# Down projection as seven products in passes over the chunks, with two weight sums formed in memory

## The chip, the cores and the metric

The kernel runs on one core of one Trainium2 chip. The metric is device microseconds of one execution; lower is better. Engines are called as the profile calls them: PE (TensorE), PEld (its weight loads), DVE (VectorE), ACT (ScalarE), POOL (GpSimd) and SP (SyncE, which issues most loads here).

## The reference

One layer of an encoder on 512 tokens of 2048 features, in float32. Three groups of attention heads read one normalised input; their output goes through a projection and is added to x. Then comes the gated MLP, the part that matters here:

```
h = rmsnorm(x, ffn_norm)                          # 512 x 2048
g = causal_dwconv(h @ w_gate, conv_w, conv_b)     # 512 x 5632, width 3
u = h @ w_up                                      # 512 x 5632
x = x + (silu(g) * u) @ w_down                    # 5632 -> 2048: "down"
return rmsnorm(x, final_norm)
```

## The kernel before, in words

Activations are kept transposed: features lie on the 128 partitions, the 512 tokens along the row. To reach float32 precision, each operand is split into a high and a low part in a reduced format (`split`, L57): ACT copies it with rounding into the high part (L58) and DVE subtracts that from the operand (L59). One product of two tiles is then three matmuls (`mm3`, L61: high times low, low times high, high times high, all at L64).

The program runs in stages. The attention stage (heads `n` = 0 to 15; the first 8 are differential, then 4 stick-breaking pairs, then 4 band pairs) weaves the small matmuls of one head with the big projections of the following head (`weave`); the order on PE is that in which the program writes them, the order on the other engines is set by a planner that places each instruction where it expects its inputs and buffers to be ready. POOL takes part in the heads: it negates the row maximum of each softmax block (L375) and masks triangles in the stick heads (L506). Then come the output projection (`wo`), gate and up, and down.

Gate and up work on 44 tiles `f` of 128 hidden features. The first four are plain products of 512 columns. The other 40 (`strassen`, L799) take the weights of gate and up and the halves of tokens and contraction as 2x2 blocks and form seven products of 256 columns in place of eight. Their weight sums are formed on the way in by accumulating loads (L808) and by DVE (L819). At the end of each `f` the result `u` (a part of the tile `g`) is multiplied with the activated gate `cv` (L881) and written to `a_dram` on POOL's queue (L882). The tiles `g`, `cv`, `U`, `X` are in the pool `fp`, the weights in the five tiles of the pool `r4`, all opened for this stage and closed at its end. Pools are stacked: one that is opened after others have closed lies on their bytes.

Down takes the 44 hidden tiles as 11 chunks of 4 (`CH`, `NCH`). `gated(c)` loads a chunk of features (1 MB) from `a_dram` into a tile of the pool `wraw` and splits it into the tiles `ah`, `al`, in the pool `big`. `down` walks over four groups `g` of weights (1 MB each, `load_unit`) and in each over four tiles of 128 output features: 4 hidden tiles x 3 matmuls of 512 columns into one PSUM bank `dn`, and one addition into `x2` (L930). `x2` holds x after attention; its eight tiles take the place of `sums_`, the input sums of the gate stage, and are loaded at the boundary on POOL's queue (L971). The tiles `h2h` and `h2l` of the pool `h2p` hold the other inputs of the gate stage (`second`). The last chunk is done in two halves of tokens, so that the final norm of the first half can begin early.

Weights pass through two raw tiles (`wraw`) and three pairs of split tiles (`wh`, `wl` of the pool `wspl`, 1024 columns each).

Of the kernel before, what the change touches and what calls it, by code (L numbers as in the profile page):

```python
# [41 lines left out]
def trunk(ctx, tc, xT, wqkv, wo, wo15, wgu, wd, par, lam4, rel, out):  # L42
# [41 lines left out]
    def att_bank(name="att"):  # L84
        return ps_att.tile([P, S], F32, tag="att", name=name)
# [152 lines left out]
    with ExitStack() as actx:  # L238
# [110 lines left out]
        def block_scores(qkh, c, i, bank):  # L349
# [4 lines left out]
            pe.matmul(bank[:, kt], q[c][:, qt], k[c][:, kt], start=True, stop=False)  # L354
            pe.matmul(bank[:, kt], q[c][:, qt], kh[c][:, kt], start=False, stop=True)  # L355

        UOFF = [0, 128, 384, 768]

        def softmax_block(qkh, c, i, bias, dst, sums, n):

            w = (i + 1) * P
            bank = att_bank("sc")
            block_scores(qkh, c, i, bank)
            mx = sm.tile([P, 1], F32, tag="mx", name="mx")
            dve.tensor_tensor_reduce(
                out=dst,
                in0=bank[:, 0:w],
                in1=bias[:, S - w : S],
                op0=ALU.add,
                op1=ALU.max,  # L370
                scale=1.0,
                scalar=NEG,
                accum_out=mx,
            )
            pool.tensor_scalar(out=mx, in0=mx, scalar1=-1.0, scalar2=None, op0=ALU.mult)  # L375
            act.activation(dst, dst, AF.Exp, bias=mx, accum_out=sums[:, n : n + 1])

        def transposed(w):
# [122 lines left out]
        def stick_pair(p, qkh, vs):  # L501
            def strictly_before(t, fill):

                for i in range(NB):
                    o = UOFF[i] + i * P
                    pool.affine_select(  # L506
                        out=t[:, o : o + P],
                        in_=t[:, o : o + P],
                        pattern=[[-1, P]],
                        compare_op=ALU.is_gt,  # L510
                        fill=fill,
                        base=0,
                        channel_multiplier=1,
                    )
# [35 lines left out]
        ready, vtiles, pending = {}, {}, []  # L550

        def unit_order():
            yield from (HEADS_AT, HEADS_AT + 1)
# [149 lines left out]
    with ExitStack() as actx:  # L703
# [31 lines left out]
        def plain(f):  # L735
# [14 lines left out]
            pool.dma_start(a_dram[:, f, :], u)  # L750

# [44 lines left out]
            )  # L796
            return parts_of(h2p, "h2", j, b, 3)

        def strassen(f, first=False):  # L799
# [72 lines left out]
            product(halves(a12), second, 2, bank2[:, lo], False, False)  # L872
            product(halves(a22), sums_, 3, bank2[:, hi], False, True)
            dve.tensor_tensor(
                out=g[:, 2 + HS : 2 + HS + S].rearrange("p (a b) -> p a b", b=HS),
                in0=bank2.rearrange("p (a b) -> p a b", b=HS),
# [2 lines left out]
            )  # L879
            cv, silu = convolved(f, g)  # L880
            dve.scalar_tensor_tensor(out=u, in0=u, scalar=-1.0, in1=cv, op0=ALU.mult, op1=ALU.mult)  # L881
            pool.dma_start(a_dram[:, f, :], u)  # L882
            return silu

        NPLAIN = 4
# [3 lines left out]
                sums_ = [sums(j) for j in range(KT // 2)]  # L889
        second = [blocks(j) for j in range(KT // 2)]  # L890
        for f in range(NPLAIN, NFT):
            silu = strassen(f, f == NPLAIN)


    with ExitStack() as actx:
        fp = actx.enter_context(tc.tile_pool(name="fp", bufs=2))
        x2 = None

        def gated(c):

            raw = wraw.tile([P, CH, S], F32, tag="raw", name="araw")
            sync.dma_start(raw, a_dram[:, c * CH : (c + 1) * CH, :])
            ah, al = [], []
            for i in range(CH // 2):
                j = (c % 2) * 2 + i
                h, l = [big.tile([P, 2, S], F32R, tag=f"b{x}{j}", name=f"a{x}") for x in "hl"]
                split(h, l, raw[:, 2 * i : 2 * i + 2, :])
                ah += [h[:, n, :] for n in range(2)]
                al += [l[:, n, :] for n in range(2)]
            return ah, al  # L910

        ssum3 = h2p.tile([P, S], F32, tag="ssum", name="ssum3")

# [49 lines left out]
                    yield  # L963
            yield

        a = gated(0)
        x2 = []
        for j in range(4, 8):
            for x in "hl":
                t = big.tile([P, 2, S], F32, tag=f"b{x}{j}", name="x2")  # L970
                pool.dma_start(t, x_dram[:, len(x2) : len(x2) + 2, :])  # L971
                x2 += [t[:, n, :] for n in range(2)]
# [7 lines left out]
        t0, t1 = slice(0, S // 2), slice(S // 2, S)  # L980

        kept = [
            [h2p.tile([P, 1024], F32R, tag=f"h2{x}{i}", name=f"k{x}{i}") for x in "hl"] for i in range(8)
        ]
        kept = [kept[2 * g : 2 * g + 2] for g in range(4)]
        down((load_unit(wd[NCH - 1, g], kept[g]) for g in range(4)), a, t0, squares)
# [72 lines left out]
```

## Time and profile before

| | |
|---|---|
| median of 3 runs | 2275.19 us (2273.24 to 2277.32) |
| profiled execution, its own time | 2275.25 us |
| its span, first to last instruction | 2273.5 us |
| mean granted PE clock | 0.99 |
| PE busy | 2215.1 us, 97% of the span |
| DVE, ACT, POOL busy | 1530.2, 993.1, 286.8 us |
| moved by DMA | 333 MB, mean 147 GB/s |

A row of a group reads: line, engine, operation, output <- inputs, shapes, xcount, then busy time and mean ns of one, then idle time of the engine just before these instructions and what ended it. A row of a window has its length, the busy time of each engine with the number of instructions, the granted clock, the share of time in which the DMA engines were busy, and GB/s. A row of a tile gives shortest, median and longest duration in ns and the start of the first and the last instruction. A row of the timeline starts with the start time and the duration. A row of DMA issues ends with KB each and the median us from issue to landing.

### The profile page before, as it was taken

What the parts mean: (1) busy time and instruction counts of PE and PEld (TensorE: products, weight loads), DVE (VectorE), ACT (ScalarE), POOL (GpSimd) and SP (SyncE); (2) the same over time, 40 slices, a digit from 0 to 9 for tenths busy, and PEclk for the clock granted to TensorE, in tenths of its full rate; (3) what the DMA queues carried; (4) which work ended last, traced back from release to release, by engine and by line L of the source; (5) the groups of instructions that cost most, each with busy time, mean ns of one, the idle gap of its engine ahead of it and who ended that gap; (6) DMA issues with size and microseconds to landing.
All of it is one profiled execution on the core that took longest, in us unless ns stands there. A gap on an engine that the chain in (4) does not pass through costs nothing.

```text
span 2273.5 us, 34753 instructions
## 1 busy us (share of the span) xinstructions
PE 2215.1 (97%) x14012; PEld 2015.8 (89%) x14012; DVE 1530.2 (67%) x2183; ACT 993.1 (44%) x1490; POOL 286.8 (13%) x519
## 2 busy tenths in 40 slices
PE   6999999989999999899999999999999999999997
PEld 6889888878888888689999999999999888888887
DVE  7675766787777547767777777777777655555565
ACT  4554555565565323344444444444444322222232
POOL 5000100221111320001111101111110000000003
PEclk9999999999999999999999999999999999999999
DMA  5222222222234444767787777777775533333332
GB/s 183 86 84 94 87 79 89 79 79 80 98 112 157 160 150 156 232 189 188 196 208 192 195 197 189 203 203 191 198 189 158 213 127 113 130 111 119 140 130 75
DMA packets 79745, 333.07 MB, mean 147 GB/s; under 512 B 9312, under 2 KB 14176, under 8 KB 63200
## 3 DMA queue, kind: packets, MB, share of 16 engines
q1 hardware_dynamic: 57776, 257.84, 34.0%
q0 software_dynamic: 20512, 71.84, 14.2%
q8 instruction: 110, 1.80, 0.3%
q10 hardware_dynamic: 1296, 1.17, 0.2%
q14 instruction: 51, 0.42, 0.1%
HBM read 307.22 MB, written 23.59 MB: 146 GB/s over the span
## 4 chain that ended last, share of the span: by engine, by line
PE 89%; DVE 5%; ACT 2%; DMA 2%; issue 1%; POOL 1%; SPq 0%; POOLq 0%; DVEq 0%; ACTq 0%
PE c L64 35%; PE dn L64 21%; PE wo L64 8%; PE v L64 7%; PE k L64 6%; PE q L64 6%; PE tr L385 1%; DMA xt<-x_dram 1%; PE g L64 1%; DVE wl L59 1%; PE pv L64 1%; PE sc L355 1%; PE sc L354 1%; DVE l L536 1%; POOL z L506 1%
## 5 line engine op out<-in xcount | busy, mean ns | idle before, releaser
L58 ACT CAST wh<-raw 128x1024 fp32r<-128x1024 f32 (+1 forms) x227 | 236.1, 1041 | 504.5 <-PE dn L64 299.8
L64 PE MATMUL c<-bl,wh 128*128 128x256 f32 x1280 | 363.5, 284 | 13.6 <-ACT wh L58 13.6
L59 DVE TENSOR_TENSOR wl<-a,wh 128x1024 fp32r<-128x1024 f32 x200 | 244.6, 1224 | 191.8 <-ACT wh L58 191.7
L64 PE MATMUL c<-bh,wl 128*128 128x256 f32 x1280 | 363.5, 284 | 0.7 <-DVE wl L59 0.7
L64 PE MATMUL c<-bh,wh 128*128 128x256 f32 x1280 | 363.3, 284 | 0.0
L59 DVE TENSOR_TENSOR wl<-raw,wh 128x1024 fp32r<-128x1024 f32 (+1 forms) x227 | 277.3, 1223 | 98.5 <-ACT wh L58 98.1
L58 ACT CAST wh<-a 128x1024 fp32r<-128x1024 f32 x200 | 209.8, 1049 | 245.1 <-DVE a L819 207.6
L64 PE MATMUL c<-h2l,wh 128*128 128x256 f32 x960 | 272.0, 283 | 0.9 <-DVE U L844 0.9
L64 PE MATMUL c<-h2h,wl 128*128 128x256 f32 x960 | 271.8, 283 | 0.0
L64 PE MATMUL c<-h2h,wh 128*128 128x256 f32 x960 | 271.8, 283 | 0.0
L64 PEld LDWEIGHTS c<-bl,wh 128*128 128x128 f32 x1280 | 246.8, 193 | 13.8 <-ACT wh L58 13.8
L930 DVE TENSOR_TENSOR x<-dn,x 128x512 f32<-128x512 f32 (+1 forms) x192 | 123.8, 646 | 187.5 <-PE dn L64 183.4
L64 PE MATMUL dn<-al,wh 128*128 128x512 f32 x640 | 249.2, 389 | 0.8 <-DVE al L59 0.7
L64 PE MATMUL dn<-ah,wl 128*128 128x512 f32 x640 | 249.0, 389 | 0.0
L64 PE MATMUL dn<-ah,wh 128*128 128x512 f32 x640 | 249.0, 389 | 0.0
L64 PEld LDWEIGHTS c<-bh,wl 128*128 128x128 f32 x1280 | 246.8, 193 | 1.0 <-DVE wl L59 1.0
L64 PEld LDWEIGHTS c<-bh,wh 128*128 128x128 f32 x1280 | 246.9, 193 | 0.0
L64 PEld LDWEIGHTS c<-h2l,wh 128*128 128x128 f32 x960 | 184.6, 192 | 1.1 <-DVE U L844 1.1
L64 PEld LDWEIGHTS c<-h2h,wl 128*128 128x128 f32 x960 | 184.5, 192 | 0.0
L64 PEld LDWEIGHTS c<-h2h,wh 128*128 128x128 f32 x960 | 184.4, 192 | 0.0
L64 PE MATMUL v<-wl,hh 128*128 128x256 f32 x512 | 149.3, 292 | 13.1 <-DVE wl L59 12.9
L64 PE MATMUL v<-wh,hl 128*128 128x256 f32 x512 | 147.6, 288 | 4.1 <-DVE hl L59 4.1
(241 smaller groups left out, 4736.4 us busy)
## 6 DMA issues: line engine op xcount, KB each, us to landing
a<-in_wgu SPq DMA_DIRECT2D x120, 512.0 KB, 4.8
raw<-in_wqkv SPq DMA_DIRECT2D x46, 1024.0 KB, 4.8
raw<-in_wd SPq DMA_DIRECT2D x44, 1024.0 KB, 4.9
z<-in_wgu SPq DMA_DIRECT2D x80, 512.0 KB, 5.8
z<-in_wgu POOLq DMA_DIRECT2D x80, 512.0 KB, 9.8
raw<-in_wo SPq DMA_DIRECT2D x16, 1024.0 KB, 4.8
a_dram<-g POOLq DMA_DIRECT2D x44, 256.0 KB, 6.0
araw<-a_dram SPq DMA_DIRECT2D x11, 1024.0 KB, 4.9
```

The source lines that it names most:

```text
L58: act.copy(out=hi, in_=src)
L59: dve.tensor_tensor(out=lo, in0=src, in1=hi.bitcast(F32), op=ALU.subtract)
L64: pe.matmul(o, l[x], r[y], start=start and i == 0, stop=stop and i == 2, skip_group_check=on)
L354: pe.matmul(bank[:, kt], q[c][:, qt], k[c][:, kt], start=True, stop=False)
L355: pe.matmul(bank[:, kt], q[c][:, qt], kh[c][:, kt], start=False, stop=True)
L385: pe.transpose(out=bank[:, (i - j) * P : (i - j + 1) * P], in_=w[:, o : o + P], identity=ident)
L506: pool.affine_select(out=t[:, o : o + P], in_=t[:, o : o + P], pattern=[[-1, P]], compare_op=ALU.is_gt, fill=fill, base=0, channel_multipl ...
L536: dve.tensor_tensor_scan(back, back, back, 0.0, ALU.add, ALU.max)
L930: dve.tensor_tensor(out=x2[m][:, t], in0=bank, in1=x2[m][:, t], op=ALU.add)
```

## The change

Down for chunks 0 to 9 is written as seven products. A pair `q` of chunks gives two column blocks of the weights; the output tiles of each group of weights give two row blocks; the tokens are halved. All products have 256 columns. Product `r` reads one combination of weight blocks and one combination of feature blocks, and is added into one to four of the four output blocks (`INTO`). The products are done in five passes over the five pairs: (5), then (6, 3) together, (4), (1, 7) together, (2). In a pass a product keeps its four PSUM banks over all five pairs, and is added into `x2` only in the last.

The weight sums s1 (row 1, both columns) and s2 (s1 plus row 0, column 0) are formed in DRAM by copies and accumulating transfers on POOL's queue during the attention stage, three a head, 40 in all. The two other sums of weights are formed by DVE. The feature combinations are formed by DVE from blocks of 128 x 1024 in a new pool `ar` of five tiles, and two of them are kept in DRAM (`t1_dram`, `t2_dram`) for later passes. Weights are loaded as two 512 KB tiles that take the places of `h2h` (eight tiles), for the first pair of the first pass as 1 MB into `wraw`. `a_dram` has a new order with the halves of tokens apart, so each write of `u` is in two runs a partition. In the last `f` of the gate stage the order of the last two products is swapped. The last chunk and the final norm are as before, save for which `h2` tiles keep its weights.

```diff
-    a_dram = dram.tile([P, NFT, S], F32, name="a_dram")
+    a_dram = dram.tile([P, 2, NFT, S // 2], F32, name="a_dram")
...
+            last_pool[:] = [pool.tensor_scalar(out=mx, in0=mx, scalar1=-1.0, scalar2=None, op0=ALU.mult).ins]
...
+        def weight_sums():
+            def block(i, row, col):
+                q, g = i // 2, i % 2 * 2
+                return wd[2 * q + col, g : g + 2, :, row * 1024 : (row + 1) * 1024]
+            n = 2 * NQ
+            for i in range(n + 2):
+                if i < n:
+                    yield lambda: pool.dma_start(s1_dram[i], block(i, 1, 0))
+                    yield lambda: pool.dma_start(s2_dram[i], block(i, 0, 0))
+                if 1 <= i < n + 1:
+                    yield lambda: pool.dma_start(s1_dram[i - 1], block(i - 1, 1, 1), accum_op=ALU.add)
+                if 2 <= i:
+                    yield lambda: pool.dma_start(
+                        s2_dram[i - 2], s1_dram[i - 2], accum_op=ALU.add, max_dma_last_dim=1024
+                    )
...
+            marks = [total * x // 4 for x in (1, 2, 3)]
             for w in att:
                 done += w
+                while marks and done >= marks[0]:
+                    marks.pop(0)
+                    issue = next(wsums, None)
+                    if issue is not None:
+                        with tc.issue_after(last_pool[0]):
+                            issue()
...
+            if last:
+                product(halves(a22), sums_, 3, bank2[:, hi], False, False)
+            product(halves(a12), second, 2, bank2[:, lo], False, last)
+            if not last:
+                product(halves(a22), sums_, 3, bank2[:, hi], False, True)
...
+        ar = actx.enter_context(tc.tile_pool(name="ar", bufs=5))
...
+        def block(c, t):
+            b = ar.tile([P, 1024], F32, tag="a", name="ab")
+            sync.dma_start(b, a_dram[:, t, c * CH : (c + 1) * CH, :].rearrange("p a b -> p (a b)"))
+            return b
...
+        def features(r, q):
+            if r in (1, 2, 3):
+                return in_parts(block(2 * q + (r > 1), int(r == 3)))
+            if r == 5:
+                x, y = block(2 * q, 0), block(2 * q, 1)
+                dve.tensor_tensor(out=x, in0=x, in1=y, op=ALU.subtract)
+                pool.dma_start(t1_dram[q], x)
+                return in_parts(x)
+            if r == 7:
+                x, y = block(2 * q + 1, 1), block(2 * q, 1)
+                dve.tensor_tensor(out=x, in0=x, in1=y, op=ALU.subtract)
+                return in_parts(x)
+            x, y = block(2 * q + 1, int(r == 6)), ar.tile([P, 1024], F32, tag="a", name="tb")
+            sync.dma_start(y, (t1_dram if r == 6 else t2_dram)[q])
+            dve.scalar_tensor_tensor(out=x, in0=x, scalar=-1.0, in1=y, op0=ALU.mult, op1=ALU.subtract)
+            if r == 6:
+                pool.dma_start(t2_dram[q], x)
+            return in_parts(x)
...
+        def raw_blocks(src, first):
+            if first:
+                raw = wraw.tile([P, 2, 1024], F32, tag="raw", name="raw")
+                sync.dma_start(raw, src.rearrange("g p n -> p g n"))
+                return [raw[:, g, :] for g in range(2)]
+            tiles = []
+            for g in range(2):
+                raw = h2p.tile([P, 1024], F32, tag=f"h2h{raws[0] % 8}", name="raw")
+                raws[0] += 1
+                sync.dma_start(raw, src[g])
+                tiles.append(raw)
+            return tiles
+
+        def weights(rs, q, g2, first):
+            def a(row, col):
+                return raw_blocks(wd[2 * q + col, 2 * g2 : 2 * g2 + 2, :, row * 1024 : (row + 1) * 1024], first)
+            i = 2 * q + g2
+            srcs = {
+                (5,): lambda: (raw_blocks(s1_dram[i], first),),
+                (6, 3): lambda: (raw_blocks(s2_dram[i], first), a(0, 1)),
+                (4,): lambda: (a(1, 1),),
+                (1, 7): lambda: (a(0, 0), a(1, 0)),
+                (2,): lambda: (a(0, 1),),
+            }[rs]()
+            for g in range(2):
+                ws = []
+                for n, src in enumerate(srcs):
+                    if n:
+                        dve.tensor_tensor(out=src[g], in0=src[g], in1=srcs[0][g], op=ALU.add)
+                    wh = wspl.tile([P, 1024], F32R, tag="wh", name="wh")
+                    wl = wspl.tile([P, 1024], F32R, tag="wl", name="wl")
+                    split(wh, wl, src[g])
+                    ws.append((wh, wl))
+                yield ws
+
+        INTO = {
+            1: ((0, 0), (0, 1), (1, 0), (1, 1)),
+            2: ((0, 0),),
+            3: ((0, 1),),
+            4: ((1, 0),),
+            5: ((0, 1), (1, 1)),
+            6: ((0, 1), (1, 0), (1, 1)),
+            7: ((1, 0), (1, 1)),
+        }
+
+        def one_pass(rs, new_banks, first=False):
+            banks = [[new() for _ in range(4)] for new in new_banks]
+            for q in range(NQ):
+                fs = [features(r, q) for r in rs]
+                for g2 in range(2):
+                    for gg, ws in enumerate(weights(rs, q, g2, first and q == 0)):
+                        g = 2 * g2 + gg
+                        for bank, f, w in zip(banks, fs, ws):
+                            # 2 output tiles x 4 hidden tiles, mm3 of 256 columns each
...
+                        if q == NQ - 1:
+                            # bank g of each product is added into x2 as INTO says
...
-        for c in range(NCH - 1):
-            down((load_unit(wd[c, g]) for g in range(4)), a)
-            a = gated(c + 1)
+        one_pass((5,), (acc,), True)
+        one_pass((6, 3), (acc, dn_bank))
+        one_pass((4,), (dn_bank,))
+        one_pass((1, 7), (acc, dn_bank))
+        one_pass((2,), (acc,))
+        a = gated(NCH - 1)
```

More of the change, by code (lines that the diff above doesn't have):

```diff
@@ L107, in trunk @@
     x_dram = dram.tile([P, KT, S], F32, name="x_dram")
-    a_dram = dram.tile([P, NFT, S], F32, name="a_dram")
+    a_dram = dram.tile([P, 2, NFT, S // 2], F32, name="a_dram")
+    NQ = NCH // 2
+    s1_dram, s2_dram = [
+        [dram.tile([2, P, 1024], F32, name=f"{n}_{i}") for i in range(2 * NQ)] for n in ("s1", "s2")
+    ]
     def feature_tiles(tag, name, dtype=F32R):
@@ L505, in strictly_before @@
                     o = UOFF[i] + i * P
[L506 to L514, printed above, removed]
+                    last_pool[:] = [
+                        pool.affine_select(
+                            out=t[:, o : o + P],
+                            in_=t[:, o : o + P],
+                            pattern=[[-1, P]],
+                            compare_op=ALU.is_gt,
+                            fill=fill,
+                            base=0,
+                            channel_multiplier=1,
+                        ).ins
+                    ]
             zs = []
@@ L897, in trunk @@
         x2 = None
+        ar = actx.enter_context(tc.tile_pool(name="ar", bufs=5))
+        HS = S // 2
+        raws, combs = [0], [0]
         def gated(c):
             raw = wraw.tile([P, CH, S], F32, tag="raw", name="araw")
-            sync.dma_start(raw, a_dram[:, c * CH : (c + 1) * CH, :])
+            for t in range(2):
+                sync.dma_start(raw[:, :, t * HS : (t + 1) * HS], a_dram[:, t, c * CH : (c + 1) * CH, :])
             ah, al = [], []
             for i in range(CH // 2):
[L905 to L909, printed above, removed]
@@ L910, in gated, with comb @@
-            return ah, al
+                h, l = comb()
+                split(h, l, raw[:, 2 * i : 2 * i + 2, :].rearrange("p a b -> p (a b)"))
+                ah += [h[:, n * S : (n + 1) * S] for n in range(2)]
+                al += [l[:, n * S : (n + 1) * S] for n in range(2)]
+            return ah, al
+        def comb():
+            j = combs[0] % 4
+            combs[0] += 1
+            return [big.tile([P, 1024], F32R, tag=f"b{x}{j}", name=f"a{x}") for x in "hl"]
+        x2p = []
@@ new lines, in block, with in_parts @@
+        def block(c, t):
+            b = ar.tile([P, 1024], F32, tag="a", name="ab")
+            sync.dma_start(b, a_dram[:, t, c * CH : (c + 1) * CH, :].rearrange("p a b -> p (a b)"))
+            return b
+        t1_dram, t2_dram = [[dram.tile([P, 1024], F32, name=f"{n}_{q}") for q in range(NQ)] for n in ("t1", "t2")]
+        def in_parts(b):
+            p = comb()
+            split(*p, b)
+            return p
+        def features(r, q):
[16 more added lines that the diff above has]
+            return in_parts(x)
@@ L982, in trunk @@
         kept = [
-            [h2p.tile([P, 1024], F32R, tag=f"h2{x}{i}", name=f"k{x}{i}") for x in "hl"] for i in range(8)
+            [h2p.tile([P, 1024], F32R, tag=f"h2{'lh'[i // 4]}{i % 4 * 2 + n}", name=f"k{n}{i}") for n in range(2)] for i in range(8)
         ]
```

38 lines of the change are left out of this document (30 added, 8 removed).

## The prediction

> **What bounds the kernel now.** I read the page's busy times first, then the windows of the stages, then the instructions of the two stages that meet at the change.
>
> ```profile
> span 2273.5 us, 34753 instructions
> ...
> PE 2215.1 (97%) x14012; PEld 2015.8 (89%) x14012; DVE 1530.2 (67%) x2183; ACT 993.1 (44%) x1490; POOL 286.8 (13%) x519
> ```
>
> ```profile
> core 0: us, PE busy (x) PEld busy (x) DVE busy (x) ACT busy (x) POOL busy (x), PEclk, DMA share, GB/s
> ...
> 46.00:380.00 334.00, 334.00 (x1918) 293.90 (x1917) 214.29 (x478) 173.88 (x347) 29.47 (x94) 1.00 0.26 89
> 380.00:560.00 180.00, 168.94 (x974) 148.62 (x973) 139.13 (x193) 109.18 (x192) 38.44 (x83) 0.97 0.22 77
> ...
> 977.00:1776.00 799.00, 797.69 (x6646) 797.29 (x6644) 581.22 (x632) 366.66 (x437) 93.43 (x155) 1.00 0.73 190
> 1776.00:2212.00 436.00, 435.63 (x1921) 360.53 (x1922) 236.79 (x269) 111.00 (x107) 3.33 (x7) 1.00 0.39 138
> ```
>
> TensorE bounds all of it. The stage that changes is 1776 to 2212 (down for ten chunks): PE is busy 435.6 of 436 us at a granted clock of 1.00, DVE 237, DMA 0.39. The gate and up stage before it (977 to 1776) already works by seven products of 256 columns. Its PE is as full, with DVE at 581 of 799 us (73%), so it is the pattern for what the new down asks of the other engines. Two tiles give the rates:
>
> ```profile
> L64 PE MATMUL dn<-al,wh x640: 389/389/500, 1776.3 to 2211.3; 128*128 128x512 f32 x160
> ...
> L64 PE MATMUL dn<-ah,wh x640: 388/389/393, 1776.8 to 2211.7; 128*128 128x512 f32 x160
> ```
>
> ```profile
> L64 PE MATMUL c<-bh,wh x1280: 279/283/420, 950.6 to 1775.3; 128*128 128x256 f32 x183
> ```
>
> ```profile
> 980.49 792.26 PE c L64 x6600
> ...
> 1778.00 462.93 PE dn L64 x2154
> ```
>
> The durations of single matmuls (389, 283 ns) overlap, so I use counts over time. Three groups of 640 start from 1776.3 to 2211.7 and fill about 435.5 us: 435.5 / 1920 = 0.2268 us for 512 columns. In the chain 6600 matmuls of 256 columns take 792.26 us: 0.1200 each, not half of 0.2268. Seven eighths of the columns is therefore 7.4% of the stage, not 12.5%.
>
> **The change part by part.**
>
> *Products.* Each of 7 products has 5 pairs of chunks x 4 groups x 2 x 4 tiles x 3 = 480 matmuls, 3360 in all. 3360 x 0.1200 = 403.3 us in place of 435.5: **-32.2 us**. The last chunk and the end are unchanged. The bounds of this term are the rates above (no stall inside: 403; a stage as full as the old one at 1/8 less would be 381, which the 256-column row excludes).
>
> *DVE and ACT inside the passes.*
>
> ```profile
> L930 DVE TENSOR_TENSOR x<-dn,x 128x512 f32<-128x512 f32 x160 | 110.4, 691 | 169.7 <-PE dn L64 165.8 <-DMA x<-x_dram 3.9
> L59 DVE TENSOR_TENSOR wl<-raw,wh 128x1024 fp32r<-128x1024 f32 x78 | 95.4, 1225 | 28.4 <-ACT wh L58 28.4
> L58 ACT CAST wh<-raw 128x1024 fp32r<-128x1024 f32 x78 | 82.2, 1056 | 304.9 <-PE dn L64 299.8 <-DMA raw<-in_wd 5.1
> ```
>
> ```profile
> L819 DVE TENSOR_TENSOR a<-a,z 128x1024 f32<-128x1024 f32 x40 | 49.0, 1225 | 1.4
> ```
>
> Weight splits go from 80 to 140 (x 1.22 = 171 us), weight sums on DVE from 0 to 40 (49 us), feature splits from 20 to 35 (43), feature sums from 0 to 20 (24, at the price of L819), additions into x2 fall from 160 to 14 x 4 = 56 (39 in place of 110). DVE: 326 of 403 us, 81%. By pass: a pair of a single product is 96 x 0.12 = 11.5 us of PE against at most 6 x 1.22 = 7.3 of DVE; a pair of a double pass, (6,3) or (1,7), is 23.0 of PE against 15 x 1.22 = 18.4 of DVE (80%), not far from the 73% that the gate stage bears with no idle PE. ACT needs 175 x 1.06 = 185. So no cost in the middle of a pass. At the end of pass (1,7) each group also brings 6 additions: 3 x 1.22 + 6 x 0.69 = 7.8 us of DVE against 5.8 of PE. Three such groups are 6 us short, of which the one weight split kept ahead (24 x 0.12 = 2.9 us) hides half: **+3 us**. Pass (6,3) with 4 additions a group is 0.7 short each, hidden.
>
> *Loads inside the passes.* 70 weight transfers' worth of 1.05 MB in place of 40, and 65 half-size ones for feature blocks and sums: 107 MB. The densest, pass (5), moves 3.67 MB in 11.5 us (319 GB/s), a double pass 6.3 MB in 23 (273). The window around the stage boundary shows the queues full:
>
> ```profile
> GB/s 15 0 0 0 0 44 146 320 364 288 4 0 0 0 15 0 0 0 87 269 437 400 430 444 390 459 393 411 401 393 346 393 379 397 430 219 98 186 386 342
> ...
> raw<-in_wd SPq DMA_DIRECT2D x4, 1024.0 KB, 7.5
> x<-x_dram POOLq DMA_DIRECT2D x8, 512.0 KB, 10.5
> ...
> a_dram<-g POOLq DMA_DIRECT2D x2, 256.0 KB, 5.1
> ```
>
> About 400 GB/s were moved for 16 slices on end, so 319 fits, and eight raw tiles hold 23 us of weights ahead. Cost 0; if the cover fails, pass (5) is paced at 3.67 MB / 400 = 9.2 us a pair, still under PE.
>
> *The boundary from gate to down.* Here I expect most of the gain to go. PE's last product ends at 1775.3 + 0.28 = 1775.6, and the first down matmul starts at 1776.3. That worked because chunk 0's features were read into `wraw` and `big`, which were free. In the new first pass every feature block goes through the new pool `ar`. It is opened after `fp` and `r4` have closed and is stacked on their bytes: the two `g`, `cv`, `U`, `X` and the five `r4` tiles. So the first load of a block waits for the last user of these. Whether it waits for its own bytes only, or for all tiles of the pools below, shows once in this trace:
>
> ```profile
> L679 POOL DMA_DIRECT2D xr<-in_xT x16 | 8.8, 553 | 22.1 <-PE pv L400 10.6 <-DMA x_dram<-xr 6.2 <-issue 2.4
> ```
>
> The first load into the pool `st2` waited for a value matmul of the attention stage, which reads the pools that `st2` replaced and no bytes of `xr`. So I take the whole pool: the last gate tile's `cv`, and its `g`, until it is written to `a_dram`. When is that?
>
> ```profile
> 1776.13 0.68 DVE L874 TENSOR_TENSOR g<-c,U 128x512 f32<-128x512 f32 x1
> ...
> 1777.87 1.53 DVE L720 SCALAR_TENSOR_TENSOR cv<-g,pt,cv 128x512 f32<-128x512 f32 x2
> 1783.33 0.69 DVE L930 TENSOR_TENSOR x<-dn,x 128x512 f32<-128x512 f32 x1 [3.93 <-DMA x<-x_dram]
> 1783.93 0.68 DVE L881 SCALAR_TENSOR_TENSOR g<-g,cv 128x512 f32<-128x512 f32 x1
> ```
>
> ```profile
> 1779.43 0.63 ACT L728 ACTIVATE cv<-cv 128x512 f32<-128x512 f32 x1 [1.70 <-DVE cv L720]
> ```
>
> ```profile
> 1774.60 2.62 POOL L971 DMA_DIRECT2D x<-x_dram  x5 [12.40 <-PE c L64]
> 1784.91 0.55 POOL L882 DMA_DIRECT2D a_dram<-g  x1 [7.69 <-DVE g L881]
> ```
>
> L881 now sits behind an x2 addition that waits for its load; that addition moves to the end of pass (5), so L881 can follow the Silu: 1780.06 + 0.68, or 5.1 us after PE's end. Then the write of `g`, 5.1 us by the row above; then SP, which held the block's load, issues it: 7.5 us (the time of a load beside the x2 loads; 512 KB alone would be less, bounds 4.8 by the page's row quoted below and 10.5 by x2); then difference, cast and split of the block, 1.22 + 1.06 + 1.22 = 3.5. PE waits 5.1 + 5.1 + 7.5 + 3.5 = 21.2 us in place of 0.7: **+20.5 us**. Low end, a hold by `cv`'s bytes alone: 5.1 + 4.8 + 3.5 = 13.4. High end, write and load both at 10.5: 29.6. Below that a gain is excluded, the gap was 0.7. What is queued behind the held load on SP is pass (5)'s other blocks; weights of pairs 0 to 2 use `wraw` and `h2h` tiles, free by 1775.6, and are split meanwhile as far as three tiles go. The swapped order of the last two products frees `sums_` some 2.9 us earlier, for x2, which nobody needs before the pass ends: 0.
>
> ```profile
> a<-in_wgu SPq DMA_DIRECT2D x120, 512.0 KB, 4.8
> ```
>
> *The sums in memory.* 40 transfers of 1 MB on POOL, at three marks a head, over 14 heads; the s1 additions wait for transfers four marks older, long landed.
>
> ```profile
> L808 POOL DMA_DIRECT2D z<-in_wgu x80 | 70.7, 1031 | 47.5 <-DMA z<-in_wgu 25.9 <-ACT wh L58 14.8 <-issue 6.7
> L375 POOL TENSOR_SCALAR mx<-mx 128x1 f32<-128x1 f32 x96 | 31.5, 328 | 221.1 <-DVE mx L365 202.0 <-DVE r L442 6.8 <-ACT vv L296 5.4
> ```
>
> Nearest price: 0.9 to 1.0 us of POOL for an accumulating transfer, 40 us in all, against POOL busy 29 of 334 and 38 of 180 in the windows above. Each may hold one negated maximum (L375), or a triangle mask in the stick heads, by 1 us; PE has projection matmuls between, and was idle 0.0 and 11 us there. DMA share 0.26 and 0.22 leaves room. Bounds 0 and +40; I take **+1**, near the lower row, as the marks lie behind the head's last POOL work. The `a_dram` write in two runs a partition costs no more than its landing, behind 18 us of other work in all but the last tile.
>
> *Sum.* -32.2 + 3 + 20.5 + 1 = -7.7. The profiled execution took 2275.25 us, 0.06 over the median 2275.19 (1.75 outside its span of 2273.5). 2275.25 - 7.7 = 2267.6; I say **2268**, 0.3% faster.
>
> **The rivals.**
> *Not held (faster).* If the block loads wait for nothing late (their part of the pool free by the last weight split), the boundary costs about nothing: 2247; with the hold by `cv` alone 2260. Against it: the `xr` row.
> *Rings drained first (no change).* x2's 4.2 MB on POOL's queue and 4.2 MB of weights for pairs 1 and 2 on SP's are issued from 3 us before PE's end; the write of `g` stands behind the one, the block behind the other. 8.65 MB at 400 GB/s is 21.6 us, so the write lands 18.6 us after PE's end; with 4.8 and 3.5 the gap is 26.9 and the time 2273. For it: x2 took 10.5 us and raw 7.5 in that window, against 4.8 in the row of the 512 KB loads. The Trainium skill, "DMA: Bandwidth & Descriptors", section "Queues, rings and completion order", says that each of 16 engines consumes one queue's ring in order and takes turns between queues; by that rule it would go this way, and the stretched landings agree.
> *DVE paces the double passes (slower).* If sum, cast and split of the second weight run one after another with nothing between (1.22 + 1.22 + 1.06 + 1.22 = 4.7 us a group, four groups, plus 3 x 2.3 for three feature splits with their casts: 25.7 against 23.0), ten pairs lose 27 us: 2295. It decides from 5.8 us of unfilled DVE waits a pair: the slack of 23.0 - 18.4 = 4.6, and 1.2 more in each of ten pairs to eat the 7.7 and 4.6 besides. Against it: the gate stage has the same depth of three tiles and the same kind of chain, and its PE does not idle.
> *POOL's transfers hold the heads (slower).* Half of 40 at 1 us: 2287.
>
> **How the numbers follow.** Chances: my forecast 0.36 (own range 2260 to 2276), not held 0.22, rings 0.20, DVE 0.13, POOL 0.09. Range 2246 to 2289. No change means within 0.2%, 4.6 us, about what a measurement of this kernel can tell: 2270.6 to 2279.7. Faster: not held, and two thirds of the forecast, 0.46; same: the rest of it and most of the rings, 0.28; slower: 0.26.
>
> **What would show it.** Right: 480 matmuls a product at 0.12 us; one PE gap of 17 to 27 us after the last `c`, ended by DVE's split of the first block, its load issued only after the last `a_dram` write; a few us at the end of pass (1,7); the attention stage within 3 us. Wrong: no gap there, or PE idle in short pieces through passes (6,3) and (1,7) ended by DVE, or POOL named in the waits of the heads.

## The result and the profile after

The changed kernel took 2365.43 us (median of 4 runs, 2357.13 to 2367.62), the kernel before beside it 2274.22 (4 runs, 2272.72 to 2277.32). The ratio is 1.0394, 95% interval 1.0378 to 1.0411: 4% slower, where 2268 had been predicted with a range of 2246 to 2289. The page of the changed kernel begins so:

```profile
span 2364.8 us, 38080 instructions
...
PE 2208.6 (93%) x15452; PEld 2072.8 (88%) x15452; DVE 1612.1 (68%) x2214; ACT 1071.7 (45%) x1565; POOL 329.8 (14%) x569
```

TensorE (PE) is as busy as before less 6.5 us, in a span that is 91.3 us longer. It has no more work; it waits, and beside its waits it is slower (last section). Four groups of its matmuls (shortest, median and longest ns of one, first and last start) show where:

```profile
L64 PE MATMUL g<-h2l,wh x64: 389/389/389, 920.9 to 997.2; 128*128 128x512 f32 x64
...
L64 PE MATMUL c<-h2h,wh x960: 279/283/415, 1034.5 to 1833.4; 128*128 128x256 f32 x192
...
L64 PE MATMUL pa<-al,wh x640: 278/283/583, 1859.4 to 2303.2; 128*128 128x256 f32 x160
...
L64 PE MATMUL pa<-ah,wh x640: 277/283/415, 1860.0 to 2303.4; 128*128 128x256 f32 x160
```

The first row is the start of the gate stage: 920.9 us, 862.4 before. **58.5 us** are lost before it, in the attention stage, which the prediction had changed by 1. The last `c` ends at 1833.4 + 0.28 = 1833.7, so the gate stage itself took as long as before. The first matmul of the passes starts at 1859.4, a gap of **25.7 us** in place of 0.7. The last one of pass (2) ends at 2303.7: 444.3 us for the ten chunks in place of 435.8, and **41.1** over the 403.2 that the products need. Of these, about 27 are idle and 14 are busy time beyond 403.2, which stands beside the pauses (last section), by the window over the passes (columns: PE busy, PEld, DVE, ACT, POOL, granted clock, DMA share, GB/s):

```profile
1859.00:2304.00 445.00, 417.36 (x3364) 410.80 (x3365) 313.34 (x297) 185.41 (x181) 4.80 (x9) 0.99 0.70 235
```

The gap, in the chain of waits:

```profile
1839.12 8.61 DMA a_dram<-g
...
1848.23 7.34 DMA ab<-a_dram
...
1855.69 1.24 DVE ab L984
```

The passes, in the waits of PE (us in total, times, longest) and of DVE:

```profile
PE pa L64 <- DVE al L59: 25.8, 1, 25.8
PE dn L64 <- DVE wl L59: 21.4, 20, 3.5
PE pa L64 <- DVE wl L59: 5.6, 10, 1.8
```

```profile
DVE raw L1031 <- DMA raw<-in_wd: 72.9, 30, 4.2
DVE wl L59 <- ACT wh L58: 35.3, 27, 2.5
```

The first PE row is the gap, the other two are 27 us of short pauses, nearly all in the double passes, each ended by a weight split. DVE itself waits longest at L1031, the sum of two raw weights: 73 us in 30 waits, each for a load. How that comes about is seen in a stretch of pass (1,7), first DVE, then SP's queue:

```profile
2127.82 1.23 DVE L1031 TENSOR_TENSOR raw<-raw 128x1024 f32<-128x1024 f32 x1 [3.96 <-DMA raw<-in_wd]
2128.96 2.35 DVE L59 TENSOR_TENSOR wl<-raw,wh 128x1024 fp32r<-128x1024 f32 x2
2134.18 1.23 DVE L1031 TENSOR_TENSOR raw<-raw 128x1024 f32<-128x1024 f32 x1 [2.86 <-DMA raw<-in_wd]
2135.32 2.35 DVE L59 TENSOR_TENSOR wl<-raw,wh 128x1024 fp32r<-128x1024 f32 x2
2140.42 1.23 DVE L1031 TENSOR_TENSOR raw<-raw 128x1024 f32<-128x1024 f32 x1 [2.74 <-DMA raw<-in_wd]
```

```profile
2130.20 12.93 SPq L1009 DMA_DIRECT2D raw<-in_wd  x5
```

As the first of two splits ends, a raw tile is free, SP issues the next load into it (2130.20), and the very next sum on DVE is over this load, which lands 4 us later. Counted in the program's order of weight splits, the sum stands four to six splits ahead of its place, in most cases six. It stands that early because the planner ordered DVE so; behind it wait splits of earlier weights. That this order is the cause is what sum_next tests below.

The attention stage has rows of the same kind. PE's waits between 46 and 620 us:

```profile
PE tr L390 <- ACT z L546: 36.9, 4, 9.2
PE tr L390 <- DVE w L452: 12.4, 8, 4.3
```

Before, the second did not exist, and the first was

```profile
PE tr L385 <- ACT z L539: 10.0, 4, 2.8
```

Over the whole stage PE waits 57.2 us, 11.1 before. The other 12 of the 58.5 us are busy time, of slower matmuls: from 380 to 560 us the granted clock is 0.91 in this kernel and was 0.97 before (columns as above).

```profile
380.00:560.00 180.00, 151.20 (x882) 133.55 (x881) 119.28 (x173) 97.53 (x173) 39.62 (x74) 0.91 0.52 135
```

In the timeline of DVE in one differential head, of the changed kernel and then of the kernel before, `r`, `pr` and `w` are the last softmax block, `rl<-tr` the splits of the transposed pieces:

```profile
301.19 0.28 DVE L59 TENSOR_TENSOR rl<-tr,rh 128x128 fp32r<-128x128 f32 x1
302.45 0.42 DVE L59 TENSOR_TENSOR rl<-tr,rh 128x256 fp32r<-128x256 f32 x1 [0.97 <-ACT rh L58]
303.58 0.56 DVE L59 TENSOR_TENSOR rl<-tr,rh 128x384 fp32r<-128x384 f32 x1 [0.71 <-ACT rh L58]
304.36 0.17 DVE L447 RECIPROCAL r<-sums 128x2 f32<-128x2 f32 x1 [0.22 <-ACT pr L381]
...
305.07 0.35 DVE L452 SCALAR_TENSOR_TENSOR w<-pr,r 128x128 f32<-128x128 f32 x1
306.85 0.69 DVE L59 TENSOR_TENSOR rl<-tr,rh 128x512 fp32r<-128x512 f32 x1 [1.43 <-ACT rh L58]
```

```profile
282.26 0.35 DVE L447 SCALAR_TENSOR_TENSOR w<-pr,r 128x128 f32<-128x128 f32 x1
...
288.43 0.28 DVE L59 TENSOR_TENSOR rl<-tr,rh 128x128 fp32r<-128x128 f32 x1
```

Before, that block was done 6 us ahead of the first transposed piece. Now it comes after the third, and PE's last transpose waits for it, in each of the eight differential heads. Of the first 700 instructions of DVE about 130 stand elsewhere than before, though the change gave DVE nothing to do in this stage. The transfers were given to POOL.

### The profile page after: what moved, and what is told of

The parts are those of the page before. It is cut to its first block, busy times and chain, and to the rows that moved or that the text cites. A ratio compares the mean times of both kernels' runs of the same rounds, so it can differ in the third digit from the quotient of the medians.

```text
span 2364.8 us, 38080 instructions
## 1 busy us (share of the span) xinstructions
PE 2208.6 (93%) x15452; PEld 2072.8 (88%) x15452; DVE 1612.1 (68%) x2214; ACT 1071.7 (45%) x1565; POOL 329.8 (14%) x569
## 4 chain that ended last, share of the span: by engine, by line
PE 75%; DVE 10%; DMA 9%; issue 2%; ACT 2%; POOL 1%; SPq 0%; DVEq 0%; POOLq 0%; ACTq 0%
PE c L64 33%; PE q L64 7%; PE wo L64 7%; PE v L64 7%; PE k L64 7%; DMA raw<-in_wd 5%; PE dn L64 4%; DVE wl L59 3%; PE pa L64 3%; DVE raw L1031 1%; PE tr L390 1%; DMA ab<-a_dram 1%; DMA tb<-t 1%; PE g L64 1%; DVE l L543 1%
## 5 line engine op out<-in xcount | busy, mean ns | idle before, releaser
L58 ACT CAST wh<-raw 128x1024 fp32r<-128x1024 f32 (+1 forms) x287 | 298.4, 1041 | 466.6 <-PE pa L64 110.3
L59 DVE TENSOR_TENSOR wl<-raw,wh 128x1024 fp32r<-128x1024 f32 (+1 forms) x287 | 347.7, 1220 | 130.9 <-ACT wh L58 130.5
L64 PE MATMUL pa<-al,wh 128*128 128x256 f32 x640 | 182.9, 286 | 25.8 <-DVE al L59 25.8
L64 PE MATMUL pa<-ah,wl 128*128 128x256 f32 x640 | 183.9, 287 | 5.6 <-DVE wl L59 5.6
L64 PE MATMUL pa<-ah,wh 128*128 128x256 f32 x640 | 182.8, 286 | 0.0
L64 PE MATMUL dn<-ah,wl 128*128 128x256 f32 x480 | 138.9, 289 | 21.6 <-DVE wl L59 21.4
```

Of the source, the lines that this page charges most:

```text
L58: act.copy(out=hi, in_=src)
L59: dve.tensor_tensor(out=lo, in0=src, in1=hi.bitcast(F32), op=ALU.subtract)
L64: pe.matmul(o, l[x], r[y], start=start and i == 0, stop=stop and i == 2, skip_group_check=on)
```

## The experiments

Eleven kernels ran. Their stages, read as above from the rows of `g`, `c`, `pa` and `dn` (an end is the last start and the length of a matmul, 0.28 us, or 0.39 before), with the time as median:

| kernel | gate starts | gap before the passes | passes | total |
|---|---|---|---|---|
| before | 862.4 | 0.7 | 435.8 | 2274 |
| after | 920.9 | 25.7 | 444.3 | 2365.4 |
| no_sums | 863.5 | 27.3 | 440.8 | 2307.9 |
| tiny_sums | 918.3 | 27.6 | 442.1 | 2365.4 |
| pinned_order | 885.1 | 25.0 | 441.1 | 2324.6 |
| pinned_bias | 863.2 | 25.6 | 447.0 | 2306.8 |
| pool_order | 917.0 | 25.3 | 443.3 | 2358.9 |
| dve_act_order | 867.7 | 25.2 | 442.4 | 2308.5 |
| sum_next | 920.5 | 26.4 | 416.8 | 2336.4 |
| late_sum | 919.2 | 26.6 | 413.1 | 2334.6 |
| boundary | 919.2 | 0 | 434.2 | 2331.1 |
| combined | 862.0 | 0 | 423.5 | 2264.5 |
| second_order | 862.3 | 0 | 409.1 | 2247.5 |

**The attention stage: the transfers' work, or the order?**

*no_sums.*

```diff
-                    issue = next(wsums, None)
-                    if issue is not None:
-                        with tc.issue_after(last_pool[0]):
-                            issue()
...
-                (5,): lambda: (raw_blocks(s1_dram[i], first),),
-                (6, 3): lambda: (raw_blocks(s2_dram[i], first), a(0, 1)),
+                (5,): lambda: (a(1, 0),),
+                (6, 3): lambda: (a(0, 0), a(0, 1)),
```

> Leaves out the forming of the two weight sums: none of the 40 transfers, and the passes (5) and (6,3) read plain weight blocks of the same size in their place. All theories of the attention stage expect the first matmul of the gate stage back at 863 us (862.58 before, 921.02 after) and a total of about 2365 - 58 = 2307 us. If the stage stays later than 870, the 58 us are not the transfers' at all.

The gate stage starts at 863.5 and the total is 2307.9. So 57 of the 58 us come with the transfers. Without them DVE, ACT and POOL stand in this stage in the order of the kernel before, instruction by instruction.

*tiny_sums.*

```diff
-                    yield lambda: pool.dma_start(s1_dram[i], block(i, 1, 0))
+                    yield lambda: pool.dma_start(s1_dram[i][:, :, 0:64], block(i, 1, 0)[:, :, 0:64])
```

(the other three kinds likewise; the last of them also loses its `max_dma_last_dim`)

> The same 40 transfers at the same places, each of 64 columns in place of 1024 (1/16 of the bytes); the passes read plain weight blocks. DVE, ACT and POOL keep the changed kernel's order in the attention stage. Theory 'order' (the transfers made the planner order DVE, ACT and POOL otherwise, and that order costs the 58 us): gate stage starts at 912 to 921, total 2355 to 2365. Rival 'POOL time' (each transfer holds maxima and masks on POOL while it is issued, 1.0 to 1.8 us): the issue gets shorter, 880 to 905. Rival 'traffic' (80 MB of memory to memory traffic make the weights late): 863 to 868, total 2307 to 2312.

918.3 and 2365.4: a sixteenth of the bytes, and 2.6 us of 58 come back. Traffic is out. POOL's time is not out by this run, since its issues got little shorter (0.97 us in place of 0.96 for the additions from the weights, 1.16 in place of 1.58 for `s<-s`), which the expectation had not foreseen.

*pinned_order.* The order in which DVE, ACT and POOL issue the stage's instructions was read from the kernel without the transfers, and each instruction was tied to the one ahead of it by an edge that orders the issue and waits for nothing. The transfers are left out of the tie, at their marks.

```diff
+        span = list(traced)[mark0:]
+        for e, moves in PLAN.items():
+            ins = [...]    # the stage's instructions of engine e, without the transfers
+            ins = [ins[k + x] for k, x in enumerate(moves)]
+            for x, y in zip(ins, ins[1:]):
+                tc.add_manual_dep(y, x.name, DependencyInfo(DependencyClass.NoSync, ...))
```

> The changed kernel with all its transfers in full size, but DVE, ACT and POOL are held to the order of the kernel before in the attention stage; the transfers stand between, at the same marks. 'Order': gate stage starts at 863 to 868, total 2307 to 2313. 'POOL time': 900 to 921, since POOL still issues 40 transfers ahead of maxima and masks. 'Traffic': 915 to 921, total 2360 to 2366, since the bytes are the same.

885.1 and 2324.6, between what any theory had said: 36 us come back with the order alone, 22.7 stay. The heads of this run keep the times of the kernel before, 1.4 us late, up to the eighth (its values start at 339.25, 337.87 before). Then two waits appear, of which this is the first, in the chain of waits and on DVE:

```profile
361.49 0.59 POOL s L622
...
362.24 0.58 POOL s L624
362.82 15.70 DMA rbias<-in_rel
```

```profile
378.58 0.11 DVE L543 MEMSET rbias<- 64x64 f32 x1 [12.95 <-DMA rbias<-in_rel]
378.72 1.23 DVE L115 TENSOR_TENSOR wl<-raw,wh 128x1024 fp32r<-128x1024 f32 x1
```

The bias of the band heads, 256 KB on POOL's queue, is issued right behind transfers of 1 MB and lands 15.7 us later; in the kernel before, the same load landed in 3.0:

```profile
rbias<-in_rel POOLq DMA_DIRECT2D x5, 256.0 KB, 3.0
```

DVE's first instruction on it then holds splits and transposes. At 599 to 614 us the same happens again. The Trainium skill, "DMA: Bandwidth & Descriptors", section "Two DMAs through the same engine are not ordered", says that within one queue of one DMA engine descriptors start in order; these 15.7 us agree with it. In the changed kernel itself these loads do not stand behind transfers: their median landing is 2.9 us, and DVE waits 0.4 us for them in all. So this wait comes with the tie, and is no part of the 58 us.

*pinned_bias.*

```diff
-                pool.dma_start(bias, rel[2 * p + c])
+                sync.dma_start(bias, rel[2 * p + c])
```

> As pinned_order, with the eight loads of the band heads' bias on SP's queue in place of POOL's. Theory 'behind in the queue' (in pinned_order a bias of 256 KB issued right behind two transfers of 1 MB landed 14 to 15 us later and DVE, then PE, waited for it twice: 885.1 against 862.4 at the start of the gate stage): the stage starts at 863 to 867, total 2303 to 2310. Rival 'POOL time or traffic' for these 22.7 us: it still starts at 880 to 886, total 2320 to 2327.

```profile
L120 PE MATMUL g<-h2l,wh x64: 389/389/389, 863.2 to 939.6; 128*128 128x512 f32 x64
```

```profile
rbias<-in_rel SPq DMA_DIRECT2D x7, 256.0 KB, 3.0
```

863.2 and 2306.8. With the order restored and the bias on another queue, 40 full transfers cost the attention stage 0.8 us. POOL's time for them, 41 us in the changed kernel, was hidden after all.

*pool_order* and *dve_act_order*: pinned_bias with only one part of the tie.

```diff
-        for e, moves in PLAN.items():           # DVE, ACT, POOL
+        for e, moves in PLAN.items():           # POOL alone / DVE and ACT alone
```

> pinned_bias with POOL alone held to the order of the kernel before; DVE and ACT keep the changed kernel's order in the attention stage. What is told apart is which engine's order costs the 55 us that tiny_sums and no_sums show. Theory 'store ahead of maxima' (POOL's store of a head's output, placed in front of the next head's first maxima, waits up to 30 us and holds them): the gate stage starts at 863 to 875, total 2304 to 2316. Rival 'DVE and ACT' (the last softmax blocks and the masks' scans stand behind the splits and transposes on DVE): it starts at 905 to 920, total 2347 to 2365.

> The counterpart: DVE and ACT held to the order of the kernel before, POOL left to the planner. 'Store ahead of maxima': start of the gate stage at 900 to 920, total 2342 to 2365. 'DVE and ACT': 863 to 875, total 2304 to 2316.

```profile
L77 PE MATMUL g<-h2l,wh x64: 389/389/390, 917.0 to 993.4; 128*128 128x512 f32 x64
```

```profile
L111 PE MATMUL g<-h2l,wh x64: 389/389/390, 867.7 to 944.1; 128*128 128x512 f32 x64
```

My theory of the store ahead of the maxima falls: with POOL's order restored 54 of 58 us are still there, with that of DVE and ACT 5 are. It had a long wait to show for itself (POOL stood up to 30 us before that store), but a wait of an engine that nobody needs costs nothing. What costs is the order of DVE and ACT. By the waits above it is the place of the last softmax block, and in the stick heads of what `z` waits for (36.9 us in place of 10.0); which of the two engines, and which of the moved instructions, was not tried apart.

**The passes: order, DVE's load, or late loads?**

*sum_next.*

```diff
-                        dve.tensor_tensor(out=src[g], in0=src[g], in1=srcs[0][g], op=ALU.add)
+                        with tc.issue_after(before[0]):    # the last split of the group before
+                            dve.tensor_tensor(out=src[g], in0=src[g], in1=srcs[0][g], op=ALU.add)
```

> In the double passes the sum of two raw weights is held on DVE behind the last split of the group before it; in the changed kernel DVE meets the sum up to eight splits earlier, when its load has only just been issued. Theory 'sum too early': the passes take 403 to 412 us in place of 444.3, total 2325 to 2335. Rival 'DVE paces' (the work of a double pass in sequence is longer than PE's 23 us): the passes still take 425 to 445, total 2347 to 2366. Rival 'loads late' (SP's order holds the raw loads back): within 5 us of 2365. The start of the gate stage and the gap of 25.7 us ahead of the passes stay in all.

The passes take 416.8 us, 27.5 less, and the total is 2336.4: both a little above what the theory had. The waits of DVE for raw loads are gone from its list; what is left first is

```profile
DVE wl L1039 <- ACT wh L1037: 72.9, 63, 2.5
```

which PE hardly feels: its short waits in the passes fall from 27 us to 5.9. The load that the sum waited for was neither late nor slow; the sum was early.

*late_sum.*

```diff
-                        with tc.issue_after(before[0]):
+                        with tc.issue_after(last_split[0]):    # the first weight's split of its own group
```

> As sum_next, but the weight sum is held on DVE behind the first weight's split of its own group, so that sum, cast and split of the second weight follow each other with nothing between. If a double pass is paced by that chain, as a rival of the prediction had it (25.7 us a pair against 23.0), the passes take 416.8 + 27 = 444 us and the total is about 2363. If the three tiles of split weights hide it, the passes stay at 415 to 420 and the total at 2334 to 2340.

413.1 us and 2334.6: no pacing by the chain of sum, cast and split. The rival "DVE paces the double passes" of the prediction falls with it.

**The boundary.**

*boundary.*

```diff
-        ar = actx.enter_context(tc.tile_pool(name="ar", bufs=5))
...
+            if n < 2:
+                if n == 0:
+                    first_blocks.append(wraw.tile([P, 2, 1024], F32, tag="raw", name="ab0"))
+                return first_blocks[0][:, n, :]
+            return h2p.tile([P, 1024], F32, tag=f"h2l{3 + n % 5}", name=name)
```

> The changed kernel without the new pool for the feature blocks: the first pair's two blocks come into a tile of wraw, the others into five h2l tiles, which only the last gate product reads; the second weights of pair 0 come into h2h tiles. Theory 'whole pool' (the first load waited for the last write to a_dram because the new pool lay over the closed ones): the gap between the last c and the first pa falls from 25.7 us to 0 to 5, and TensorE's clock no longer drops behind it (0.90 in the first 27 us of the passes where the gap stood), 2 to 4 us more; total 2335 to 2342. Rival 'rings' (the loads queue behind x2 and the weights whatever tiles they use): a gap of 12 us or more stays, total 2350 or more. The stalls inside the passes and the attention stage stay in both.

```profile
1832.57 0.28 PE L64 MATMUL c<-h2h,wh 128*128 128x256 f32 x1
1832.69 0.28 PE L64 MATMUL pa<-al,wh 128*128 128x256 f32 x1
```

No gap at all, so the loads wait for nothing but the tiles that they are given. The passes take 434.2 us, 10 less than in the changed kernel, and the total is lower than either theory had it. DVE waits 51 us there for raw loads in place of 73: the planner placed the first sums of this kernel later. PE's short waits are 20.0 us in place of 27.0, which is 7 of the 10 us; the clock is not the reason, since in these passes it is at half for 13.7 us, and for 12.1 in the changed kernel (last section).

**All together.**

*combined* is pinned_bias, sum_next and boundary in one.

> pinned_bias, sum_next and boundary together. If the three places are independent: 2365.4 - 58 (attention stage) - 27.5 (passes, 444.3 to 416.8) - 27 (gap and clock) = 2253 us, between 2246 and 2262, and so below the kernel before (2273.5). If a cured stall only uncovers another (DVE at 314 of 417 us in the passes, queues at 0.96 to 1.01 in the first pass), 2263 to 2285.

2264.5 us, ratio to the kernel before 0.9958 (0.9942 to 0.9975). Faster, but by the second of the two cases: the passes take 423.5, not 417 less the clock. Two of its windows (columns as above):

```profile
1776.00:1800.00 24.00, 19.30 (x144) 18.55 (x143) 11.12 (x11) 9.87 (x10) 1.77 (x3) 0.93 1.03 409
1800.00:1834.00 34.00, 33.73 (x281) 33.52 (x280) 25.51 (x23) 17.33 (x17) 2.13 (x4) 1.00 1.03 413
```

Without the gap, the 4.2 MB of x2 fall on pass (5), the pass with the densest loads, and the queues are full for 58 us, in which PE idles 5.0. That is a part only of the 20 us over 403.2.

*second_order.*

```diff
-        one_pass((5,), (acc,), True)
-        one_pass((6, 3), (acc, dn_bank))
-        one_pass((4,), (dn_bank,))
-        one_pass((1, 7), (acc, dn_bank))
-        one_pass((2,), (acc,))
+        one_pass((2,), (acc,), True)
+        one_pass((5,), (dn_bank,))
+        one_pass((6, 3), (acc, dn_bank))
+        one_pass((1, 7), (acc, dn_bank))
+        one_pass((4,), (dn_bank,))
...
+                                if r == 1:
+                                    later.append(lambda r=r, b=bank[g], g=g: into_x2(r, b, g))
...
+                    for _ in range((0, 1, 1, 2, 0)[q] if first else 0):
+                        tc.keep_in_program_order(sync.dma_start(*x2_loads.pop(0)))
```

> combined with the passes in the order (2), (5), (6,3), (1,7), (4), x2 loaded by SP between the weights of pairs 1 to 3 of the first pass, product 1's additions put off into pass (4), and the weight sum as in late_sum. In combined the passes still took 423.5 us against 403.2: DMA share 1.03 from the start to 1834 us, where x2, the two blocks a pair of pass (5) and its t1 stores meet, and 3.8 us of idle PE at the end of (1,7). If the queues were the cause: passes at 404 to 410 us, total 2246 to 2254. If DVE (314 of 417 us) or the roundtrip of t1 through memory was: 415 to 424, total 2256 to 2266.

2247.5 us, ratio 0.9884 (0.9869 to 0.9899): 1.2% faster than the kernel before. The passes take 409.1 us. How the 14.4 us that combined had more are shared between its edits (order of the passes, loads of x2, additions of product 1, place of the sum) was not tried. In the chain the first pass is one piece, and over it the queues still run full, without holding PE:

```profile
1775.62 57.60 PE pa L120 x480
```

```profile
1776.00:1834.00 58.00, 58.00 (x485) 58.00 (x485) 35.07 (x34) 28.10 (x28) 1.24 (x2) 1.00 1.00 392
```

## Why the prediction was wrong, step by step

*The sums in memory, +1: this step failed, by 57 us.* What it costed, POOL's time and room in the queues, was right: pinned_bias shows 0.8 us. What it took for granted was that the engines' order would stay. It costed 40 instructions on POOL as if they were put into the finished kernel, but the planner orders all engines anew around them, and DVE and ACT lost their order (55 us between no_sums and tiny_sums; 5 are left when these two have it back). The bias loads behind a transfer in the DMA queue, which the step did not name either, cost 22 us in pinned_order, and nothing in the changed kernel. The rival "POOL's transfers hold the heads", with 20 us for half of 40 issues, had neither mechanism, and its sign did not come: the waits of PE name ACT and DVE, not POOL.

*DVE and ACT inside the passes, "no cost in the middle": failed, by 27 to 31 us.* DVE's load was smaller than forecast (313 of 445 us, 70%, against 326 of 403, 81%), and late_sum shows that it can bear the passes. The step reasoned from shares of time and from the depth of the split tiles; it had no line for the place of the new sum on an engine that issues in order. The prediction's list of what would show it wrong had the sign (PE idle in short pieces through (6,3) and (1,7), ended by DVE), but with the rival's cause, not this one. The rival's own price was too high: it counts three feature splits a pair, and a double pass has two and a sum, so by its rows a pair takes 24.7 us, not 25.7.

*The boundary, +20.5: right in mechanism, short by 4.5 us (25.0 more than before, not 20.5).* `g` is ready 5.1 us after PE's end, as predicted. The write took 8.6 us in place of 5.1, the load 7.3 in place of 7.5, the difference, cast and split up to the first matmul 3.7 in place of 3.5; 0.9 more lies between them, in issues. So the term that was mis-sized is the write, beside queues that are full (DMA share 1.03 in the gap). Whether the first block waits for all that lay below the new pool, as the prediction took it, or for `g` alone, is not shown: boundary moves the blocks away from both. The rival "rings drained first" had 26.9 us, close to 25.7, by such stretching, and in part by luck: the write landed 14.0 us after PE's end, not 18.6, and the load took 7.3, not 4.8. boundary shows that without the hold the full queues make no gap.

*Products, -32.2: right.* 480 matmuls take 57.60 us in every pass that does not stall, 0.1200 each.

*Loads inside the passes, 0: nearly right.* In pass (5) of the changed kernel PE waits 3.0 us for splits, with a DMA share of 0.96; the passes behind it moved 216 GB/s at 0.65 and had room. The step did not count x2: its 4.2 MB fell into the gap here, and where the gap is cured, in combined, PE idles 4.7 us of the first 24 at a share of 1.03.

*End of pass (1,7), +3: right.* In sum_next, where nothing else pauses there, PE idles 3.65 of 37 us:

```profile
2180.00:2217.00 37.00, 33.35 (x255) 32.14 (x254) 31.86 (x38) 13.03 (x13) 0.00 (x0) 0.95 0.42 137
```

The rival "not held" had given 2247 us, for a boundary at no cost and nothing else amiss. That boundary could be had, but only with the other edits beside it did the time come to 2247.5; that the two numbers agree is luck.

## What to carry to other kernels

Where a planner orders the engines, an added instruction is not only its own duration: compare the order of every engine before and after, in the stages that were not touched too, ahead of any sum over durations. On an engine that issues in order, ask of each new instruction when its last operand can be there at the earliest, and what stands behind it; a sum of two loads that is issued early waits for a landing, whatever the busy share says. And behind bulk transfers in a DMA queue, a small load can land as late as they do (15.7 us here in place of 3.0): where somebody waits for it, give it another queue.

## What the runs showed of the hardware

A pause costs TensorE more than its length. After the gap, matmuls started every 0.21 us for 5 us, and 0.12 us apart again from 1864.7. Windows of the changed kernel (columns as above; the granted clock is the third from the end):

```profile
1859.00:1864.70 5.70, 5.27 (x24) 5.27 (x25) 3.87 (x4) 1.05 (x1) 0.96 (x2) 0.50 0.96 346
1864.70:1886.00 21.30, 20.49 (x167) 19.88 (x166) 15.10 (x13) 10.10 (x10) 1.71 (x4) 1.00 0.97 347
1912.50:1915.90 3.40, 1.57 (x13) 1.36 (x12) 2.99 (x3) 1.04 (x1) 0.00 (x0) 0.99 0.79 292
1915.90:1919.30 3.40, 3.40 (x18) 3.40 (x17) 3.40 (x5) 0.00 (x0) 0.00 (x0) 0.50 0.87 266
2154.80:2158.20 3.40, 1.71 (x15) 1.51 (x14) 2.67 (x3) 1.04 (x1) 0.00 (x0) 1.00 0.67 251
2158.20:2161.60 3.40, 3.40 (x30) 3.40 (x30) 0.83 (x1) 0.60 (x1) 0.00 (x0) 1.00 0.66 213
```

Within the passes the clock is at half three times: behind the gap, and for 3.4 us each from 1915.9 and from 2130.9, 12.1 us in all. In the trace the times of these changes (1837.3, 1864.7, 1915.9, 1919.3, 2130.9, 2134.3) lie whole multiples of 3.41 us apart. So it is not the length of a pause alone that counts, but how much of such a step it fills. The step that ends at 1915.9 has 1.83 us idle, and half the clock follows; the one that ends at 2158.2 has 1.69, and the clock stays. A longer pause, 2.27 us at 2017.3, falls on two steps, and the clock stays too. The Trainium skill, "TensorE: Matmul & The Clock Gate", section "Part 1: The HAM clock gate (the "warmup" mystery)", says that the clock is half after at least one idle window of about 3.4 us, and full after about 3.4 us of sustained work, by windows that run freely. The steps and the 3.4 us at half the clock agree with these rows; that a whole window must be idle does not, since 1.83 us were enough.

At half the clock a matmul follows the one ahead by 0.21 us in place of 0.12, so 12.1 us cost about 5 of the 14 us by which PE's 417.4 us in the passes exceed 403.2. The rest stands at the 32 pauses: the last matmul ahead of a pause counts to its end, 0.28 us in place of 0.12, and the second matmul behind a pause starts about 0.22 us after the first in place of 0.12: together about 8 us.

An addition in memory of 1 MB cost POOL 0.96 us when its source was the weights, 1.58 us for `s<-s`, and with a sixteenth of the columns 0.97 and 1.16, so the issue hardly follows the bytes.
